# Scoring order of the forget-attention tiles, late rows of the out projections, and a third v buffer

## The chip, the core and the metric

The kernel runs on one core of one Trainium2 chip. The metric is device microseconds of one execution, lower is better. One launch computes both layers; weights, activations and scratch tensors lie in HBM, and everything is moved by DMA that SyncE (SP) issues.

## The reference, cut to what matters

The trunk has 1024 tokens, model width 1024, 16 heads of 64, and two layers.

```
x = x + (fox(h) * silu(gate)) @ w_out      # layer 1, h = rms_norm(x)
x = x + (dsw(h) * silu(gate)) @ w_out      # layer 2
fox:  c = cumsum(log_sigmoid(f_logit));  s = q k^T / 8 + c_i - c_j,  causal softmax, @ v
dsw:  three groups (window, dilation) = (128,1), (512,4), (2048,16): rotary, banded
      softmax in each group, groups combined by the softmax of their log-sum-exps
```

In layer 1 the 128 queries of tile t (t = 0 to 7) see the keys of tiles 0 to t, so tile 7 has eight times the score work of tile 0. In layer 2 a tile sees its own and at most one more tile of keys.

## The kernel before, in words

Each projection multiplies a 128-token tile by a 1024 x 384 weight piece: eight k blocks, each with three matmuls (input high part times weight high part, times weight low part, input low part times weight high part), 24 matmuls in all (`project`, L308 to L316). After every second k block `flow.tick()` runs; a tick is the kernel's clock, here called a **slot**. A tile of a projection is four slots, a head pair (eight tiles) is 32.

TensorE's instructions stay in the order in which the program emits them. What isn't projection is hung on slots by `flow.at(slot, fn)`, and so lands between two pairs of k blocks. The other engines and SP get their order from a planner in the compiler, by priority and by when it expects operands and a free buffer.

Layer 1 runs the gate projections, then eight head pairs (L716 to L743), then the out projection in three column parts (L746 to L772). For a head pair, every two tiles `heads_pair` (L396 to L425) norms q and k, splits them into fp16 high and low parts `hl`, and SP transposes them by DMA into `qk_t`. `fox_tile` (L615 to L691) then scores a tile: matmuls `s` (L442), bias, maximum and copy to `p` on DVE (L644), exp on ACT (L487), fp16 high part on ACT (L490) and low part on POOL (L493) into `ph`, a DMA transpose to `ptt` (L494), and, some slots later, `values`: the matmuls with v (L501 to L503), divided and gated on DVE into `y` (L674, L680), which goes to `y_d` in HBM. Tiles 0 to 3 have one transpose for both heads, tiles 4 to 7 one for each head. There are two `ph` and three `ptt` buffers, four of `p`, two of v (`vt`).

Counted from the first slot of its head pair, tile t is scored at slot 4t+20 (the second head of tiles 4 to 7 two slots later), and its values come 8 slots and then 2 to 4 later (`lpf`, `fox`): in tiles 0 to 3 12 slots after scoring, in tiles 4 to 7 10 slots after the scoring of each head. So the tiles of a head pair are spread evenly in time, whatever their number of keys, and its last ones fall into the next head pair. The next weights are loaded and split meanwhile (`ahead`, L294); a small matmul of theirs (`scale`, L270) is hung on slot 28.

In the last head pair scoring is up to three slots earlier (`ahead`, L602). There the values are multiplied straight into the row buffer `yts[t]`, whose other columns were loaded from `y_d` (`load_y`), and both halves of the row are transposed on TensorE (`y_ready`, `transpose_half`), copied to `xh` by ACT (L325) and to `xl` by DVE (L326), two and three slots after the values. Only then may the out projection of tile t start, at slot 32+4t of the last head pair. Layer 2 ends in the same way.

Of the kernel before, what the change touches and what calls it, by code (L numbers as in the profile page):

```python
# [22 lines left out]
P = 128  # L23
# [59 lines left out]
def trunk(ctx, tc, ins, out, cfg):  # L83
# [56 lines left out]
    par_i = sb.tile([P, P], I32, name="par_i", tag="n2k", bufs=cfg["nb"])  # L140
    nc.gpsimd.iota(par_i, [[1, P]], base=P, channel_multiplier=-1)
    nc.vector.tensor_single_scalar(par_i, par_i, 1, ALU.bitwise_and)
    par = const.tile([P, P], F32, name="par")
    nc.vector.tensor_scalar(par, par_i, NEG, None, ALU.mult)
    nc.gpsimd.affine_select(par, par, [[-1, P]], ALU.is_ge, NEG, base=0, channel_multiplier=1)

# [92 lines left out]
    under = {}  # L239

# [78 lines left out]
    def transpose_half(row, h, t, own=False):  # L319
        pt = ps_o.tile([P, 512], F32, name="pt", tag="o") if own else ps_pj.tile([P, 512], F32, name="pt", tag="pj")  # L320
        for j in range(4):
            nc.tensor.transpose(pt[:, j * P : (j + 1) * P], row[:, j * P : (j + 1) * P], ident)  # L322
        pv = pt.rearrange("p (k s) -> p k s", k=4)
        dh = xh[:, 4 * h : 4 * h + 4, t * P : (t + 1) * P]
        nc.scalar.copy(dh, pv)  # L325
        nc.vector.tensor_sub(xl[:, 4 * h : 4 * h + 4, t * P : (t + 1) * P], pv, dh.bitcast(F32))  # L326
# [69 lines left out]
    def heads_pair(gi, t, hd):  # L396
# [55 lines left out]
    def v_tile(vs):  # L452
        vt = sb.tile([P, NT, 2, 129], F16, name="vt", tag="vt")
# [111 lines left out]
    zt = const.tile([P, NT, NH], F32, name="zt")  # L565

    def forget_logits(t, ps):
# [3 lines left out]
        a = sm.tile([P, NT, NH], F32, name="fa", bufs=1)  # L571
# [28 lines left out]


    def ahead(hp, t):  # L602
        if hp < NHP - 1:
            return cfg["lsf"], cfg["lpf"]
        n = cfg["lsf"] - t // 2
        return n, (22 if t < 4 else 21) - n

    bcs = {}

    def load_bc(hp, h):  # L610
        for e in range(2):
# [3 lines left out]
    def fox_tile(hp, t, gs, kts, vt, e0):  # L615
        LS, LP = ahead(hp, t)
# [8 lines left out]
        def score(e, c):  # L625
            a, b = pieces[c]
            if c == 0:
# [43 lines left out]
        def finish():  # L671
            o = st["o"]
            rec = sm.tile([P, 2], F32, name="rec", tag="rec")
            nc.vector.reciprocal(rec, o[:, :, HD])  # L674
            if hp == NHP - 1:
                y = yts[t][1][:, 384:]
            else:
                y = sb.tile([P, P], F32, name="y", tag="y")
            for e in range(2):
                nc.vector.scalar_tensor_tensor(y[:, e * HD : (e + 1) * HD], o[:, e, :HD], rec[:, e : e + 1], gs[:, e * HD : (e + 1) * HD], ALU.mult, ALU.mult)  # L680
            if hp == NHP - 1:
                y_ready(t, flow.now)
# [4 lines left out]
        ts, tv = cfg["fox"][2 * (hp == NHP - 1) + both]  # L687
# [6 lines left out]
    yts = {}  # L694
    turned = set()

    def load_y(t, g):
        yts[t] = rows2("yt")
        nc.sync.dma_start(yts[t][0], y_d[tile_rows(g, t), :512])
# [311 lines left out]
```

## Time and profile before

| what | value |
|---|---|
| time, median of 3 runs (lowest, highest) | 1839.21 us (1836.2, 1841.85) |
| the profiled execution, and its span | 1839.68 us, 1837.9 us |
| PE busy | 1763.5 us, 96% |
| DVE, ACT, POOL busy | 1097.0, 987.9, 953.1 us (60%, 54%, 52%) |
| chain of waits, by engine | PE 51%, DMA 21%, DVE 9%, issue 7%, POOL 6%, ACT 5% |
| projections L313, x8448 | 2393.4 us of busy time (they overlap) |

PE is TensorE's matmuls, PEld its weight loads, SPq the DMA queue that SP issues. The page's strip of 40 slices shows PE at 9 tenths in almost all of them; the head pairs of layer 1 lie in the fourth to thirteenth slice, where the strip of the DMA engines stands at 7 to 9.

### The profile page before, as it was taken

The page shows a single profiled execution, that of the slowest core. Times are in us where ns is not written, and L with a number is a line of the kernel's source. Part 1 is how long each engine was busy: PE and PEld are TensorE (multiplying, and loading weights), DVE is VectorE, ACT ScalarE, POOL GpSimd, SP SyncE. Part 2 cuts the span into 40 slices and gives each one's busy share as a digit, 9 for nine tenths or more (in the row PEclk, how much of TensorE's full clock was granted, in tenths as well). Part 3 has the DMA queues.
Part 4 walks back from the last instruction along what each step waited for, and adds up shares of the span by engine and source line. Part 5 has one row for each costly group of instructions (what it writes and reads, how often), then busy time and mean ns, then how long its engine had stood idle before and what let it go on. Part 6 is the DMA issues. An engine that isn't in the chain of part 4 may idle for free.

```text
span 1837.9 us, 39161 instructions
## 1 busy us (share of the span) xinstructions
PE 1763.5 (96%) x13784; PEld 1695.6 (92%) x13784; DVE 1097.0 (60%) x3762; ACT 987.9 (54%) x2648; POOL 953.1 (52%) x1163
## 2 busy tenths in 40 slices
PE   6999999999998899999999999999999999999999
PEld 5999889888887889999999999999999999999999
DVE  8546666576654363355555666666666766667641
ACT  6536656566664254455555565555555555555520
POOL 4215555565553121155565655666676766757620
PEclk9999999999999999999999999999999999999999
DMA  8447888888889464356767687667666766668752
GB/s 273 118 127 155 182 174 183 186 168 177 193 185 202 128 221 135 94 123 137 144 129 143 134 201 142 132 157 151 142 148 152 167 143 145 151 133 186 175 168 92
DMA packets 631430, 289.27 MB, mean 157 GB/s; under 512 B 510000, under 2 KB 594992, under 8 KB 631232
## 3 DMA queue, kind: packets, MB, share of 16 engines
q1 hardware_dynamic: 631232, 286.77, 69.2%
q8 instruction: 108, 1.77, 0.4%
q14 instruction: 90, 0.74, 0.1%
HBM read 124.87 MB, written 37.03 MB: 88 GB/s over the span
## 4 chain that ended last, share of the span: by engine, by line
PE 51%; DMA 21%; DVE 9%; issue 7%; POOL 6%; ACT 5%; SPq 2%; POOLq 0%; ACTq 0%; DVEq 0%
PE pj L313 44%; DMA ptt<-ph 6%; DMA raw<-in_w_dsw 4%; PE s L442 3%; DMA raw<-in_w_fox 3%; DMA qk_t<-hl 3%; POOL w L291 2%; DMA x_d<-xo 1%; POOL hl L421 1%; POOL ph L493 1%; DMA og_d<-og 1%; ACT ph L490 1%; DVE w L291 1%; ACT w L289 1%; PE pt L322 1%
## 5 line engine op out<-in xcount | busy, mean ns | idle before, releaser
L313 PE MATMUL pj<-w,xh 128*128 128x384 f32 (+2 forms) x5632 | 1450.9, 340 | 35.7 <-ACT w L289 11.9
L313 PEld LDWEIGHTS pj<-w,xh 128*128 128x128 f32 x5632 | 1004.1, 191 | 48.6 <-ACT w L289 12.9
L313 PE MATMUL pj<-w,xl 128*128 128x384 f32 (+2 forms) x2816 | 942.5, 335 | 0.1
L313 PEld LDWEIGHTS pj<-w,xl 128*128 128x128 f32 x2816 | 537.9, 191 | 0.9 <-DVE xl L326 0.9
L291 POOL TENSOR_TENSOR w<-raw,w 128x384 fp32r<-128x384 f32 (+2 forms) x264 | 265.4, 1026 | 349.3 <-ACT w L289 330.0
L493 POOL TENSOR_TENSOR ph<-p,ph 128x512 f16<-128x512 f32 (+3 forms) x176 | 173.0, 999 | 161.5 <-ACT ph L490 116.4
L289 ACT CAST w<-raw 128x384 fp32r<-128x384 f32 (+2 forms) x352 | 162.6, 500 | 123.0 <-PE pj L313 50.7
L421 POOL TENSOR_TENSOR hl<-u,hl 128x512 f16<-128x512 f32 x128 | 150.9, 1179 | 120.5 <-ACT hl L420 119.7
L823 POOL TENSOR_TENSOR ph<-p,ph 128x768 f16<-128x768 f32 (+2 forms) x96 | 155.5, 1619 | 106.5 <-ACT ph L822 104.0
L376 ACT ACTIVATE sq<-pj 128x256 f32<-128x256 f32 x256 | 97.4, 380 | 188.4 <-DVE u L371 186.8
L442 PE MATMUL s<-qk_t 128*128 128x128 f16 (+1 forms) x1504 | 163.9, 249 | 15.7 <-DMA qk_t<-hl 11.2
L501 PEld LDWEIGHTS <-ptt 128*128 128x128 f16 x1136 | 103.8, 99 | 43.1 <-issue 28.6
L258 DVE TENSOR_REDUCE vm<-raw 128x1 f32<-128x256 f32 x128 | 53.7, 419 | 148.7 <-DMA raw<-in_w_dsw 115.7
L487 ACT ACTIVATE p<-p,acc 128x512 f32<-128x512 f32 (+2 forms) x192 | 108.9, 608 | 56.6 <-DVE acc L644 56.6
L442 PEld LDWEIGHTS <-qk_t 128*128 128x128 f16 x1504 | 109.7, 98 | 32.0 <-DMA qk_t<-hl 14.0
L420 ACT CAST hl<-u 128x512 f16<-128x512 f32 x128 | 79.1, 618 | 102.7 <-DVE u L418 85.5
L490 ACT CAST ph<-p 128x512 f16<-128x512 f32 (+3 forms) x176 | 89.6, 536 | 71.3 <-DMA ptt<-ph 69.4
L371 DVE TENSOR_TENSOR u<-pj,gr 128x256 f32<-128x256 f32 x256 | 106.3, 415 | 19.5 <-PE pj L313 19.5
L818 ACT ACTIVATE p<-p,og 128x128 f32<-128x128 f32 (+1 forms) x256 | 97.5, 441 | 33.2 <-DVE og L817 33.1
L502 PEld LDWEIGHTS <-ptt 128*128 128x128 f16 x1136 | 106.8, 98 | 0.9 <-issue 0.9
L422 DVE COPY hl<-hl 128x512 f16<-128x512 f16 x128 | 67.1, 524 | 66.8 <-POOL hl L421 66.3
L503 PEld LDWEIGHTS <-ptt 128*128 128x128 f16 x1136 | 106.8, 98 | 0.0
(167 smaller groups left out, 2260.6 us busy)
## 6 DMA issues: line engine op xcount, KB each, us to landing
raw<-in_w_dsw SPq DMA_DIRECT2D x96, 384.0 KB, 3.8
raw<-in_w_fox SPq DMA_DIRECT2D x32, 384.0 KB, 3.7
og_d<-og SPq DMA_DIRECT2D x64, 132.0 KB, 3.3
cmb<-og_d SPq DMA_DIRECT2D x64, 132.0 KB, 3.0
bc<-c_d SPq DMA_DIRECT2D x32, 256.0 KB, 5.1
gs_d<-ge SPq DMA_DIRECT2D x32, 192.0 KB, 2.7
xt<-in_xt SPq DMA_DIRECT2D x16, 256.0 KB, 4.4
xrow<-in_x SPq DMA_DIRECT2D x16, 256.0 KB, 4.5
```

The source lines that it names most:

```text
L289: nc.scalar.copy(w[:, 0, :n], raw[:, k % 2, :n])
L291: eng.tensor_sub(w[:, 1, :n], raw[:, k % 2, :n], w[:, 0, :n].bitcast(F32))
L313: nc.tensor.matmul(ps[:, :n], a[:, k, cols], w.slabs[k][:, j, :n], start=(k == 0 and i == 0), stop=(k == KT - 1 and i == 2))
L371: nc.vector.tensor_mul(u[:, t % 2].rearrange("p (a b) d -> p a b d", a=2), ps[:, : 4 * HD].rearrange("p (a b d) -> p a b d", a=2, b=2), gr ...
L421: nc.gpsimd.tensor_sub(hl[:, :, :4, 1], u, hl[:, :, :4, 0])
L442: nc.tensor.matmul(s[:, c0 : c0 + cnt * P].rearrange("p (c s) -> p c s", c=cnt), qk[:, i, blk], kk[:, j : j + cnt, e], start=(h == 0), sto ...
L487: nc.scalar.activation(p, p, AF.Exp, bias=acc, scale=-1.0)
L490: nc.scalar.copy(ph[:, e, 0, cols], p)
L493: (nc.gpsimd if pool_l else nc.vector).tensor_sub(ph[:, e, 1, cols], p, ph[:, e, 0, cols])
L502: nc.tensor.matmul(o[:, e, :HD], hi, vt[:, j, e, :HD], start=False, stop=False, skip_group_check=True)
L503: nc.tensor.matmul(o[:, e, :], lo, vt[:, j, e, HD:], start=False, stop=(b == n - 1), skip_group_check=True)
L823: nc.gpsimd.tensor_sub(ph[:, 1], st["p"], ph[:, 0])
```

## The change

Tiles of layer 1 are scored at slots out of a table, `due`, in the order 0, 1, 4, 2, 5, 3, 6, 7 with 4, 2, 4, 2, 4, 4, 8 and 4 slots behind each; in the last head pair all are at 4t+20, with values 8 slots and then 2 to 4 later, as elsewhere. Each tile loads its own piece of the gate (`gsf`), three buffers of one tile in place of three of two. The DMA transpose of q and k is put four slots behind the arithmetic. The rows of `c` (`bc`) are loaded at other slots.

Rows of the earlier head pairs are loaded and transposed ahead (`turn_y`, seven of eight blocks, PSUM from the pool of the attention outputs); the last head pair's block is transposed alone (`turn_last`), and `project` demands it only before its last two k blocks. `vt` gets a third buffer. Layer 2 has three `qk_t` buffers in place of four, the mask `par` is built at the start of layer 2, and two small tiles share another's buffers.

```diff
-    def project(w, cols):
+    def project(w, cols, last=None):
         for k in range(KT):
+            assert k < KT - 2 or last is None or last in turned
@@ heads_pair
-        qk_t = lay([P, 12, P], F16, name="qk_t", tag="qk_t")
-        nc.sync.dma_start_transpose(qk_t, hl.rearrange("p i a b d -> p (i a b d)"))
-        return qk_t.rearrange("p (i a) s -> p i a s", i=2)
+        def turn():
+            qk_t = lay([P, 12, P], F16, name="qk_t", tag="qk_t")
+            nc.sync.dma_start_transpose(qk_t, hl.rearrange("p i a b d -> p (i a b d)"))
+            return qk_t.rearrange("p (i a) s -> p i a s", i=2)
+        return turn
@@ v_tile
-        vt = sb.tile([P, NT, 2, 129], F16, name="vt", tag="vt")
+        vt = lay([P, NT, 2, 129], F16, name="vt", tag="vt")
@@ fox_tile
+            if e == 0 and c == 0:
+                gs = st["gs"] = lay([P, P], F32, name="gsf", tag="gsl")
+                nc.sync.dma_start(gs, gs_d[t * P : (t + 1) * P, hp * P : (hp + 1) * P])
...
             if hp == NHP - 1:
-                y_ready(t, flow.now)
+                turn_last(y, t, flow.now + 2)
...
-                urgent(lambda e=e, c=c: score(e, c), "ps", e0 + LS + ts[e * len(pieces) + c])
-            urgent(lambda e=e: values(e), "pv", e0 + LS + LP + tv[e])
+                urgent(lambda e=e, c=c: score(e, c), "ps", sl + ts[e * len(pieces) + c])
+            urgent(lambda e=e: values(e), "pv", sl + LP + tv[e])
+    def turn_y(t, g, slots):
+        for h, (n, (s0, s1)) in enumerate(zip((4, 3), slots)):
+            def load(h=h, n=n, s1=s1):
+                yt = lay([P, 512], F32, name="yt", tag="ga")
+                nc.sync.dma_start(yt[:, : n * P], y_d[tile_rows(g, t), 512 * h : 512 * h + n * P])
+                flow.at(s1, lambda: transpose_rows(yt, 4 * h, n, t, True))
+            flow.at(s0, load)
+    def turn_last(y, t, s):
+        def go():
+            transpose_rows(y, KT - 1, 1, t)
+            turned.add(t)
+        flow.at(s, go)
@@ loop over head pairs
-                    kts.append(heads_pair(0, t - 1, hd))
+                    turn = heads_pair(0, t - 1, hd)
+                    flow.at(flow.now + 4, lambda turn=turn, kts=kts: kts.append(turn()))
-                    fox_tile(hp, t - 1 + i, gsl[:, i], kts, vt, flow.now - 4 + 4 * i)
+                    fox_tile(hp, tt, kts, vt, s0 + (cfg["due"][tt] if hp < NHP - 1 else 4 * tt + 20))
             if hp == NHP - 1:
-                flow.at(flow.now + sum(ahead(hp, t)) - 3, lambda t=t: load_y(t, 0))
+                a = max(flow.now + 6, s0 + cfg["due"][t] - 4 * NT + cfg["lpf"] + 9)
+                turn_y(t, 0, [(a, a + 6), (a + 2, a + 8)])
@@ CFG
+ bc=((1, 0, 26), (1, 1, 28), (0, 0, 38), (0, 1, 46)), due=(29, 33, 39, 45, 35, 41, 49, 57)
- lsd=(..., (12, 9)), l1=dict(..., qk_t=6), l2=dict(..., qk_t=4, og=3)
+ lsd=(..., (12, 10)), ty2=((0, 4), (1, 5)), l1=dict(..., qk_t=6, vt=3, gsl=3)
+ l2=dict(..., qk_t=3, og=3, vt=3, gsl=3, par=1)
```

## Rows read from the trace of the kernel before

**Rows 1.** The page's first part: engine, busy us, share, instructions.

```profile
PE 1763.5 (96%) x13784; PEld 1695.6 (92%) x13784; DVE 1097.0 (60%) x3762; ACT 987.9 (54%) x2648; POOL 953.1 (52%) x1163
```

**Rows 2.** Stretches: length; busy PE, PEld, DVE, ACT, POOL; granted clock, DMA share, GB/s.

```profile
112.00:488.00 376.00, 354.75 (x3284) 332.49 (x3283) 239.37 (x846) 227.49 (x571) 206.79 (x206) 0.97 0.82 171
488.00:549.00 61.00, 58.40 (x561) 53.75 (x559) 36.87 (x129) 39.57 (x98) 37.13 (x39) 0.97 0.85 188
549.00:605.00 56.00, 47.03 (x442) 40.99 (x441) 30.33 (x97) 24.05 (x50) 17.77 (x19) 0.94 0.88 184
...
785.00:1745.00 960.00, 945.42 (x7226) 920.20 (x7225) 618.89 (x2269) 538.25 (x1549) 610.19 (x812) 1.00 0.70 149
```

**Rows 3.** Waits of PE, 112 to 488 us: total us, times, longest.

```profile
PE o L501 <- DMA ptt<-ph: 10.7, 6, 3.9
PE s L442 <- DMA qk_t<-hl: 6.2, 6, 2.8
PE s L442 <- DVE acc L644: 4.2, 6, 2.4
```

**Rows 4.** Timeline of PE: start, us, what, idle before it and its releaser.

```profile
225.90 0.94 PE L442 MATMUL s<-qk_t 128*128 128x256 f16 x8 [1.81 <-DMA qk_t<-hl]
...
255.84 0.24 PE L501 MATMUL o<-vt,ptt 128*128 128x65 f16 x1 [3.88 <-DMA ptt<-ph]
...
424.35 0.20 PE L501 MATMUL o<-vt,ptt 128*128 128x65 f16 x1 [1.80 <-DMA ptt<-ph]
```

**Rows 5.** Timeline of PE: the matmul that is hung on slot 28.

```profile
257.15 0.35 PE L270 MATMUL pj<-vm,ones 128*128 128x4 f32 x1
```

**Rows 6.** Stretches behind the three gaps of rows 4, with the granted clock.

```profile
224.00:228.00 4.00, 2.19 (x20) 2.03 (x17) 2.65 (x11) 3.42 (x10) 1.88 (x3) 1.00 0.82 172
...
254.00:262.00 8.00, 6.16 (x45) 5.92 (x46) 4.66 (x21) 3.72 (x9) 2.62 (x3) 0.57 0.61 142
...
424.00:430.00 6.00, 5.65 (x49) 5.56 (x50) 4.57 (x22) 4.31 (x11) 3.22 (x3) 0.72 0.44 103
```

**Rows 7.** Waits of ACT, 112 to 605 us, and its timeline near 570 us.

```profile
ACT ph L490 <- DMA ptt<-ph: 69.4, 42, 3.8
...
570.13 1.03 ACT L490 CAST ph<-p 128x512 f16<-128x512 f32 x2 [3.77 <-DMA ptt<-ph]
...
571.07 1.06 ACT L325 CAST xh<-pt 128x512 fp32r<-128x512 f32 x2
```

**Rows 8.** The stretch ahead of the gap at 255.84 us.

```profile
240.00:247.00 7.00, 7.00 (x91) 6.64 (x88) 2.27 (x12) 3.49 (x8) 3.31 (x4) 1.00 1.15 228
```

**Rows 9.** Transposes of the probabilities, line L494.

```profile
DMA to landing us min/median/max: 2.3/3.7/7.2
```

**Rows 10.** Waits of PE, 488 to 605 us.

```profile
PE pj L313 <- ACT xh L325: 3.9, 1, 3.9
PE pj L313 <- DVE xl L326: 3.2, 1, 3.2
PE s L442 <- DMA qk_t<-hl: 2.8, 2, 2.6
PE pt L322 <- DVE yt L680: 1.1, 1, 1.1
PE pt L322 <- DVE u L418: 0.5, 1, 0.5
```

**Rows 11.** Timeline of DVE ahead of the wait for `xl`.

```profile
596.61 0.75 DVE L196 TENSOR_SCALAR rt<-rt_pf 128x24 f32<-128x24 f32 x8 [0.19 <-issue]
...
599.16 0.68 DVE L326 TENSOR_TENSOR xl<-pt,xh 128x512 fp32r<-128x512 f32 x1
```

**Rows 12.** Waits of SP's queue over the span.

```profile
SPq L731 <- DVE y L680: 12.5, 7, 2.3
```

**Rows 13.** The chain that ended last: one tile of a projection.

```profile
804.34 4.22 PE pj L313 x24
```

**Rows 14.** Waits of PE in layer 2, 785 to 1745 us.

```profile
PE pj L313 <- DVE u L418: 6.3, 7, 1.3
```

More of the change, by code (lines that the diff above doesn't have):

```diff
@@ L319, in transpose_half, with transpose_rows @@
     def transpose_half(row, h, t, own=False):
+        transpose_rows(row, 4 * h, 4, t, own)
+    def transpose_rows(row, k0, n, t, own=False):
         pt = ps_o.tile([P, 512], F32, name="pt", tag="o") if own else ps_pj.tile([P, 512], F32, name="pt", tag="pj")
-        for j in range(4):
+        for j in range(n):
             nc.tensor.transpose(pt[:, j * P : (j + 1) * P], row[:, j * P : (j + 1) * P], ident)
-        pv = pt.rearrange("p (k s) -> p k s", k=4)
-        dh = xh[:, 4 * h : 4 * h + 4, t * P : (t + 1) * P]
+        pv = pt[:, : n * P].rearrange("p (k s) -> p k s", k=n)
+        dh = xh[:, k0 : k0 + n, t * P : (t + 1) * P]
         nc.scalar.copy(dh, pv)
-        nc.vector.tensor_sub(xl[:, 4 * h : 4 * h + 4, t * P : (t + 1) * P], pv, dh.bitcast(F32))
+        nc.vector.tensor_sub(xl[:, k0 : k0 + n, t * P : (t + 1) * P], pv, dh.bitcast(F32))
     def inv_sqrt(y, v, n, a):
@@ L564, in trunk @@
     nc.sync.dma_start(bfb, b_f.partition_broadcast(P))
-    zt = const.tile([P, NT, NH], F32, name="zt")
+    zt = lay([P, NT, NH], F32, name="zt", tag="p")
     def forget_logits(t, ps):
@@ L570, in forget_logits @@
             return
-        a = sm.tile([P, NT, NH], F32, name="fa", bufs=1)
+        a = lay([P, NT, NH], F32, name="fa", tag="p")
         nc.vector.scalar_tensor_tensor(a, zt, -1.0, zt, ALU.mult, ALU.max)
@@ L598, in urgent, with load_bc, fox_tile @@
         flow.at(slot, go)
[L602 to L606, printed above, removed]
     bcs = {}
-    def load_bc(hp, h):
-        for e in range(2):
+    def load_bc(hp, h, es=(0, 1)):
+        for e in es:
             bcs[hp, e, h] = lay([P, 512], F32, name="bc", tag="ga")
             nc.sync.dma_start(bcs[hp, e, h], c_d[2 * hp + e, h * 512 : (h + 1) * 512].partition_broadcast(P))
-    def fox_tile(hp, t, gs, kts, vt, e0):
-        LS, LP = ahead(hp, t)
+    def fox_tile(hp, t, kts, vt, sl):
+        LP = cfg["lpf"]
         nk = (t + 1) * P
@@ L674, in finish @@
             nc.vector.reciprocal(rec, o[:, :, HD])
+            y = sb.tile([P, P], F32, name="y", tag="y")
+            for e in range(2):
+                nc.vector.scalar_tensor_tensor(y[:, e * HD : (e + 1) * HD], o[:, e, :HD], rec[:, e : e + 1], st["gs"][:, e * HD : (e + 1) * HD], ALU.mult, ALU.mult)
             if hp == NHP - 1:
[L676 to L680, printed above, removed]
@@ L694, in trunk @@
[L694 to L699, printed above, removed]
-        nc.sync.dma_start(yts[t][1][:, :384], y_d[tile_rows(g, t), 512 : D - P])
-    def y_ready(t, s):
-        def go(h):
-            transpose_half(yts[t][h], h, t)
-            if h == 1:
-                del yts[t]
-                turned.add(t)
-        for h in range(2):
-            flow.at(s + 2 + h, lambda h=h: go(h))
+                urgent(lambda e=e, c=c: score(e, c), "ps", sl + ts[e * len(pieces) + c])
@@ L720, in trunk @@
             load_bc(0, 0)
-        flow.at(s0 + ahead(hp, NT - 1)[0] + 5, lambda hp=hp: load_bc(hp, 1))
-        if hp + 1 < NHP:
-            flow.at(s0 + 20, lambda hp=hp: load_bc(hp + 1, 0))
+        for h, e, slot in cfg["bc"]:
+            if hp + 1 - h < NHP:
+                flow.at(s0 + slot, lambda n=hp + 1 - h, h=h, e=e: load_bc(n, h, (e,)))
         kts = []
@@ L789, in dsw_pair @@
     def dsw_pair(g, t0, qks, vt, done, get, LSD, LPD):
-        mask = par if g == 2 else None
+        mask = masks.get(g)
         look, at = [], [0]
@@ L864, in combine @@
         t0 = t - CB + 1
+        y2 = lay([P, N2, HD], F32, name="y2", tag="gsl")
+        nc.vector.tensor_mul(y2, y, gv)
         if hp == NHP - 1:
             for i in range(CB):
-                nc.vector.tensor_mul(yts[t0 + i][1][:, 384:].rearrange("p (e d) -> p e d", e=2), y[:, 2 * i : 2 * i + 2], gv[:, 2 * i : 2 * i + 2])
-                y_ready(t0 + i, flow.now + 2 * i)
-        else:
-            y2 = sb.tile([P, N2, HD], F32, name="y2", tag="gsl", bufs=cfg["gb"])
-            nc.vector.tensor_mul(y2, y, gv)
+                turn_last(y2.rearrange("p (t e) d -> p t (e d)", e=2)[:, i], t0 + i, flow.now + 3 + i)
+        else:
             nc.sync.dma_start(
@@ L882, in load_cmb @@
         assert all((hp, g, i) in written for g, i in [(0, i) for i in range(NT)] + [(2, t // 2), (2, t // 2 + 4)])
[L883 removed]
+        cmb[1] = lay([P, CB, P], F32, name="gsd", tag="gsl")
         for gg in range(2):
@@ L942, in trunk @@
                     for i in range(2):
-                        flow.at(flow.now + LSD + LPD - 3 + 2 * i, lambda t=t0 + i: load_y(t, 1))
+                        turn_y(t0 + i, 1, [(flow.now + a + 2 * i, flow.now + b + 2 * i) for a, b in cfg["ty2"]])
         w = w2
```

35 lines of the change are left out of this document (17 added, 18 removed).

## The prediction

> **What bounds the kernel now.** I read the page's first part, then a table of stretches, then the waits of PE in each stretch, then the timeline at the longest gaps. The reader is to see four things.
>
> First, PE is the bound: 96% of the span is matmuls [rows 1], so this change can only win back PE's gaps and what a gap costs behind it. The stretches say where they are [rows 2]. The head pairs of layer 1 but the last (112 to 488 us) have 376.00 - 354.75 = 21.3 us of gaps; the last (488 to 549) 2.6; the first part of the out projection (549 to 605), into which the attention's tail reaches, 9.0; and layer 2 (785 to 1745) only 14.6 in 960.
>
> Second, a gap is paid twice in layer 1. The granted clock, 1.00 in layer 2, is 0.97, 0.97 and 0.94 in those three stretches. It has two levels, 2.4 and 1.2 GHz, so a mean of 0.97 over 376 us means 0.03 x 376 = 11.3 us of matmul time lost (the rounding of the column leaves 2 us either way); 0.03 x 61 = 1.8 and 0.06 x 56 = 3.4 in the others. Behind the gap at 255.84 us, 3.88 us long, the clock is 0.57 over 8 us: 0.43 x 8 = 3.4 us more [rows 4, 6]. In all 32.6 + 4.4 + 12.4 = 49.4 us can be won back.
>
> Third, the gaps of the first stretch have three releasers: transposed probabilities 10.7 us, six times, about once for each head pair; transposed q and k 6.2; and the score's PSUM tile, held until DVE has copied it out, 4.2 [rows 3]. Which tile is late follows from the slots. Behind the gap at 255.84 us come attention matmuls with v and then, at 257.15, the small matmul that is hung on slot 28 [rows 4, 5]; at that slot the code has the values of tile 7 of the pair before, second head (50 + 8 + 2 - 32 = 28). The gap at 225.90, ahead of eight score matmuls, is tile 6's (four 256-column matmuls, then two of 256 and two of 128, for seven blocks of keys; the listing merges them): it wants the keys that left the projection 12 slots earlier.
>
> Fourth, why they are late. ACT waits 69.4 us, 42 times, to write `ph` because its two buffers still sit in a transpose [rows 7]; the longest landing of one is 7.2 us against a median of 3.7 [rows 9]. In 240 to 247 us, ahead of the longest gap, the DMA share is 1.15 while DVE is busy 2.27 of 7 us [rows 8]; over the head pairs it is 0.82 [rows 2]. So the chain behind the scores is full for part of each head pair and slack for the rest.
>
> **The change part by part.** *The scoring order.* Let the chain serve 36 key blocks in 32 slots, 1.125 a slot (the average it must serve). Before, tile t brings t+1 blocks every four slots: the backlog right after tiles 4, 5, 6, 7 is 5, 6.5, 9 and 12.5 blocks, the last worth 11.1 slots. Values of these tiles come 10 slots after scoring, so tile 7 alone is late, by a slot; the gap at slot 28 is such a one. After, in the order 0, 1, 4, 2, 5, 3, 6, 7 the backlogs are 4.8, 2.3, 5, 3.5, 7.3, 6.8, 9.3 and 8.3 blocks: at most 8.2 slots. I let 9.7 of the 10.7 us go. Tile 6's keys get 17 slots in place of 12; but tile 4's now get 11 in place of 12, and their transpose is put four slots later in SP's order, into slots 28 to 31, where tile 7's transposes are. Two thirds go: 4.1 of 6.2. Waits on the copies from PSUM fall by half, as light tiles come between heavy ones: 2.1 of 4.2. Together 15.9 of 21.1, three quarters; the same share of the clock loss is 8.5. Term: -24.4, bounds -32.6 and 0; how it could lose is the last rival.
>
> Of the clock I take the average, and a rule says it isn't sure. A gap of 1.81 us was free (clock 1.00 behind it), one of 1.80 us was charged 0.28 x 6 = 1.7 us [rows 4, 6]. The Trainium skill, "TensorE: Matmul & The Clock Gate", section "Part 1: The HAM clock gate", has the gate watch activity on a free-running beat, so that equal gaps may fare differently. If this holds, gaps that shrink may keep their charge; that is the first rival.
>
> *The last head pair and the out projection.* In the last head pair I change nothing: its own tiles keep one every four slots, behind the late tiles 6 and 7 of the pair before. In 549 to 605 us two waits are 7.1 of 8.9 us [rows 10], and both are in-order queues: ACT reaches the copy to `xh` at 571.07 only after a `ph` copy that sat 3.77 us behind a transpose [rows 7]; DVE reaches `xl` at 599.16 after the rotary tables, from 596.61 on [rows 11]. After, each tile has one such hand-over in place of two, with a quarter of the columns: transpose at slot 4t+34, wanted before the last k block. Between them lie nine matmuls, 9 x 4.22 / 24 = 1.6 us [rows 13]; the first half now has one slot, 1.06 us. The queues ahead are the same, so an unlucky one still costs. I halve the three waits on `xh`, `xl` and `yt`, 8.2 us, and the clock loss: -4.1 - 1.7. Against it, tail tiles are scored two or three slots later: by the same count the backlog at tile 7 is 18.4 blocks, not 15.9. Values ran there without a wait for a transpose, so the tail serves at least 1.5 a slot (15.9 in about 10 slots); 2.5 blocks more are 1.7 slots, 1.8 us. Term: -4.0, bounds -12.4 and +6 (another wait like the one at 571 us, 3.9, with its share of the clock, 1.7).
>
> *At nothing.* The third `vt` buffer: values of tile 7 now reach slot 69, past the start of the pair after next at 64; without it that pair's v would wait. PE shows no wait for it in layer 1 before [rows 3], so nothing is gained either. The gate loads and the other split rows cost SP and ACT instructions; ACT is busy 227.49 of 376 and 24.05 of 56 us [rows 2], and gates are wanted 10 slots after they are issued. If that cover fails it is the slow rival below. The mask leaves the first microseconds for the end of the gate projections, where it has a layer's length of slack. Three `qk_t` in layer 2: a pair of tiles is scored 16 slots after its heads and serves as keys eight slots later, so its buffer is free at 24, when the fourth pair asks. The largest wait of PE in layer 2, 6.3 us, is for DVE reading out PSUM [rows 14], which no part touches. Layer 2: 0, with 4 either way for the planner's new order, under the 14.6 us of gaps there.
>
> **Sum.** -24.4 - 4.0 = -28.4, from 1839.7 for the profiled execution, 0.5 above the median of the runs: 1811.3, so 1811 us. If a gap goes, nothing else is late next but PE itself.
>
> **The rivals.** *Gaps shrink, the clock stays low.* Half of the first stretch's 21.3 us goes, none of the 11.3, and the tail gives 3: 1839.7 - 10.6 - 3 = 1826. For it: 1.80 us was enough to be charged. Against: most waits have a clear cause that goes.
>
> *All of it goes.* First stretch and tail: 1839.7 - 32.6 - 12.4 = 1795. Against: tile 4's keys have a slot less.
>
> *Order doesn't matter.* If the chain is bound by its sum (two `ph` buffers in use through the whole head pair), spreading gives nothing and only the tail moves: 1838. For it, 42 waits on `ph` [rows 7]; against, a DMA share of 0.82 on average.
>
> *Slower: gate loads block SP.* With the new table four tiles are under way at slots 39 to 45 (1, 4, 2, and 0 or 5), and a gate buffer is held from scoring to the values; there are three. A load whose buffer is still held waits at the head of SP's queue, and all transposes behind it wait too: two slots for tile 2 (39 to 41, when tile 0's values are through), four for tile 5 (to 45), two each for tiles 3 and 6, ten in all. A slot is about 56 / 32 = 1.7 us there. If half of them are lost ahead of tile 5's and 3's transposes, values come 7.3 + 5 - 10 = 2.3 slots late: 4 us and 1.7 of clock in each of seven head pairs, 40 us, against 24.4 + 4.0 gained: 1851. It decides if SP loses over about three slots a head pair. For it: SP already waits 12.5 us for gate buffers [rows 12]. Against: the planner may put the transposes ahead of the load, since the gate is wanted 10 slots later.
>
> **How the numbers follow.** Forecast 0.50; gaps shrink 0.20; all goes 0.10; order doesn't matter 0.07; slower 0.13. The forecast's own range, with the bounds of its terms, is 1801 to 1822. Down to 1795 and up to 1834 the range takes in the first two rivals and leaves out the last two, 2 in 10. About 0.3%, 5.5 us, can be told from no change: faster 0.50 + 0.20 + 0.10 = 0.80, within 0.07, slower 0.13.
>
> **What would show it.** Right: from the first to the seventh head pair PE waits for transposed probabilities at most twice, not six times; gaps there near 5 us and the clock at 0.99; in the out projection's first part one gap over 2 us at most. Wrong: SP waiting over 2 us at the gate load in most head pairs (slower); waits of `s` for `qk_t` once a head pair at tile 4; many gaps of 1 to 2 us with the clock still at 0.97 (gaps shrink); or ACT's wait for `ph` unchanged near 69 us with PE's gaps as before (order doesn't matter). Gaps in layer 2 beyond 19 us would say that its buffers were not free after all.

## The result, and the profile after

The changed kernel takes 1827.26 us (median of 7 runs, 1826.13 to 1831.49) against 1841.85 us (7 runs of the kernel before beside it): ratio 0.9929, 95% interval 0.9912 to 0.9946. It is faster, by some 13 us. The forecast was 28.4 us: the sign was right, the size less than half. The median of the kernel before went from 1831 to 1842 us from chip to chip, so from here on kernels are compared by their ratio to the kernel before on the same chip.

The page's first part of the profiled execution after (1826.89 us, span 1825.1), to set beside [rows 1]:

```profile
PE 1755.6 (96%) x13784; PEld 1689.7 (93%) x13784; DVE 1103.3 (60%) x3774; ACT 988.5 (54%) x2664; POOL 953.9 (52%) x1163
```

The stretches that answer to [rows 2]: length; busy PE, PEld, DVE, ACT, POOL; granted clock, DMA share, GB/s.

```profile
112.00:480.00 368.00, 348.31 (x3237) 326.14 (x3235) 243.80 (x839) 224.04 (x563) 205.58 (x203) 1.00 0.87 172
480.00:541.00 61.00, 57.80 (x560) 52.74 (x561) 41.05 (x132) 43.34 (x105) 35.98 (x36) 0.97 0.98 201
541.00:597.00 56.00, 48.84 (x508) 44.64 (x507) 30.64 (x101) 25.37 (x59) 21.52 (x23) 0.93 0.90 197
775.00:1735.00 960.00, 948.23 (x7252) 922.12 (x7250) 620.86 (x2278) 542.39 (x1561) 610.51 (x813) 1.00 0.70 151
```

The reader is to see that the head pairs still have 368.00 - 348.31 = 19.7 us of gaps (21.3 before), but that their clock is 1.00 and no longer 0.97. The tail's clock is as low as before. A window with nearly the same work in both says it more exactly: from the first arithmetic on q and k of the first head pair to that of the eighth. First before, then after:

```profile
122.00:493.10 371.10, 349.85 (x3268) 327.38 (x3267) 235.48 (x839) 224.98 (x566) 206.36 (x206) 0.97 0.83 173
```

```profile
123.00:485.20 362.20, 342.41 (x3220) 319.83 (x3220) 239.63 (x833) 221.96 (x561) 204.68 (x204) 1.00 0.88 174
```

Seven head pairs take 371.1 - 362.2 = 8.9 us less. Of these 349.85 - 342.41 = 7.4 are PE's busy time, and only 1.5 are gaps. Not all of the 7.4 is the clock: with the later slots more of the seventh head pair's attention falls behind the window, 39 value matmuls and 14 score matmuls, and 5 more projection matmuls lie in it. At the 0.03, 0.09 and 0.18 us that such matmuls stand apart in PE's timeline, that is some 1.5 us (an estimate), which leaves 6 for the clock. The span is 12.8 us shorter: 1.0 is lost ahead of this window; the tail from there to the first gate projection of layer 2 gives 3.1 (PE starts that one 11.0 us earlier, at 672.82 us for 683.78, and the eighth head pair's arithmetic 7.9 earlier); layer 2 gives 1.8.

Which waits made the gaps? PE's waits in 112 to 480 us after, to set beside [rows 3]:

```profile
PE o L504 <- DMA ptt<-ph: 11.5, 10, 1.9
PE s L445 <- DVE acc L642: 5.0, 10, 1.0
```

The wait for transposed q and k is gone (6.2 before). The wait for transposed probabilities is not: 11.5 us in ten pieces, after 10.7 in six. It was cut into shorter pieces. Who waited for `ptt`, after, over the whole span (total us, times):

```profile
ACT ph L493: 61.4, 36
...
PE o L504: 14.3, 11
```

Before, ACT's number was 69.4 [rows 7], so the ring of `ph` buffers is nearly as crowded as it was. Two gaps in PE's timeline, and the stretches that hold them (the granted clock is the third number from the end), show what shorter pieces can save:

```profile
368.87 0.20 PE L504 MATMUL o<-vt,ptt 128*128 128x65 f16 x1 [1.94 <-DMA ptt<-ph]
...
480.10 0.24 PE L504 MATMUL o<-vt,ptt 128*128 128x65 f16 x1 [2.78 <-DMA ptt<-ph]
```

```profile
366.00:376.00 10.00, 7.12 (x87) 6.39 (x86) 5.59 (x19) 5.66 (x16) 4.61 (x6) 1.00 1.03 218
476.00:484.00 8.00, 5.22 (x45) 4.65 (x44) 3.48 (x11) 3.17 (x10) 3.57 (x5) 0.79 1.02 211
```

Behind 1.94 us the clock stays at 1.00; behind 2.78 it falls to a mean of 0.79 over 8 us, another 1.7 us. Length alone doesn't decide. In e15_ypj (below), whose head pairs have the same code, the same wait was 1.91 us long and was charged 0.21 x 8 = 1.7 us:

```profile
368.60 0.20 PE L504 MATMUL o<-vt,ptt 128*128 128x65 f16 x1 [1.91 <-DMA ptt<-ph]
```

```profile
368.00:376.00 8.00, 7.40 (x80) 7.10 (x81) 3.85 (x18) 5.74 (x16) 4.64 (x5) 0.79 0.91 221
```

Yet short pieces come off better on the whole. In the changed kernel and in nine runs below that keep its order and two `ph` buffers (e2, e3, e4, e5, e7, e8, e9, e15, e16), PE's longest wait in 112 to 480 us is 1.5 to 2.9 us and the clock is 1.00, in e15_ypj 0.99; in e1_even, with waits up to 4.1 us, it is 0.97. So what the change gained in the head pairs it gained mostly on the clock, with shorter gaps, and hardly on the gaps themselves.

PE's waits in the tail, 480 to 600 us, to set beside [rows 10]:

```profile
PE pt L321 <- DVE xl L325: 3.9, 3, 3.5
PE pt L321 <- issue: 2.8, 2, 1.6
PE o L504 <- DMA ptt<-ph: 2.8, 1, 2.8
PE pj L309 <- DVE xl L325: 2.5, 1, 2.5
PE pt L321 <- DMA yt<-y_d: 1.1, 1, 1.1
```

The two waits of 7.1 us on `xh` and `xl` are one of 2.5, but the rows transposed ahead have waits of their own (`pt`, 7.8 us).

### The profile page after: what moved, and what is told of

The parts are those of the page before. It is cut to its first block, busy times and chain, and to the rows that moved or that the text cites. A ratio compares the mean times of both kernels' runs of the same rounds, so it can differ in the third digit from the quotient of the medians.

```text
span 1825.1 us, 39283 instructions
## 1 busy us (share of the span) xinstructions
PE 1755.6 (96%) x13784; PEld 1689.7 (93%) x13784; DVE 1103.3 (60%) x3774; ACT 988.5 (54%) x2664; POOL 953.9 (52%) x1163
## 4 chain that ended last, share of the span: by engine, by line
PE 53%; DMA 17%; DVE 10%; ACT 7%; POOL 6%; issue 5%; SPq 1%; POOLq 0%; DVEq 0%; ACTq 0%
PE pj L309 47%; DMA raw<-in_w_dsw 4%; DMA ptt<-ph 4%; PE s L445 3%; POOL w L285 2%; DMA raw<-in_w_fox 2%; POOL ph L496 2%; DMA qk_t<-hl 2%; DVE p L642 2%; POOL hl L420 1%; ACT p L490 1%; DMA x_d<-xo 1%; ACT ph L493 1%; PE pt L321 1%; DVE u L417 1%
## 5 line engine op out<-in xcount | busy, mean ns | idle before, releaser
L504 PEld LDWEIGHTS <-ptt 128*128 128x128 f16 x1136 | 103.6, 98 | 44.3 <-issue 25.1
L388 DVE TENSOR_REDUCE pj<-sq 128x8 f32<-128x512 f32 x128 | 88.4, 691 | 47.5 <-ACT sq L375 47.4
L370 DVE TENSOR_TENSOR u<-pj,gr 128x256 f32<-128x256 f32 x256 | 106.5, 416 | 11.4 <-PE pj L309 11.2
L421 DVE COPY hl<-hl 128x512 f16<-128x512 f16 x128 | 61.7, 482 | 78.7 <-POOL hl L420 78.6
L505 PEld LDWEIGHTS <-ptt 128*128 128x128 f16 x1136 | 106.3, 97 | 1.8 <-issue 1.8
```

What stands on the lines that cost most here:

```text
L370: nc.vector.tensor_mul(u[:, t % 2].rearrange("p (a b) d -> p a b d", a=2), ps[:, : 4 * HD].rearrange("p (a b d) -> p a b d", a=2, b=2), gr ...
L504: nc.tensor.matmul(o[:, e, :], hi, vt[:, j, e, HD:], start=(b == 0), stop=False, skip_group_check=True)
L505: nc.tensor.matmul(o[:, e, :HD], hi, vt[:, j, e, :HD], start=False, stop=False, skip_group_check=True)
```

## The experiments

Each was timed against the kernel before in five rounds. The texts quoted name theories by letters: A, the order of scoring is what gains; B, it is worth nothing; C, the values are merely asked for too early; E, the transposes of q and k stand ahead of late probabilities in SP's order; J, other engines serve q and k in between as well; H, SP's queue is the limit; I, the DMAs' bytes are; K, the new tail is worth little; D, M and N, the number of buffers of `ph`, `ptt` or `p` is the limit. L stands for two things: in e11_ph3 to e13_p6 the serial work behind the scores, in e15_ypj the copies on DVE.

**The order alone.** Every tile of layer 1 is scored at the old slots again, all else as after.

```diff
- due=(29, 33, 39, 45, 35, 41, 49, 57)
+ due=(20, 24, 28, 32, 36, 40, 44, 48)
```

> The changed kernel with one part undone: tiles of all head pairs are scored evenly again (due = 20, 24, ..., 48); the split rows, the late transposes of q and k and the third v buffer stay. Theory A (the order is what raised the clock from 0.97 to 1.00 and closed the waits for q and k): back to about 1838, waits of s for qk_t of some 6 us and a clock near 0.97 in the head pairs. Rival B (the late transposes of q and k did it, by freeing SP's queue): stays at 1827 +- 3, no qk_t waits, clock 1.00.

Ratio 0.9988 (0.9976 to 1.0001): nearly all of the gain is gone. PE's waits, 112 to 480 us:

```profile
PE s L445 <- DMA qk_t<-hl: 14.8, 6, 4.1
PE s L445 <- DVE acc L642: 4.7, 5, 1.5
PE o L504 <- DMA ptt<-ph: 4.1, 3, 3.4
```

The order is worth 0.6%, about 11 us, and A stands. What returns is not the wait for probabilities but that for keys, in six long pieces, and more of it than before the change (6.2); here the transposes of q and k are asked for four slots later. From the first arithmetic on q and k to that of the eighth head pair it is

```profile
124.00:501.10 377.10, 351.21 (x3280) 328.86 (x3279) 235.81 (x838) 225.93 (x566) 204.75 (x206) 0.97 0.81 169
```

so 377.1 us, where the kernel before takes 371.1 and the changed one 362.2. Undoing the order alone thus gives a kernel that is 6 us worse there than the one before, and the 0.6% holds that too. The new order with the transposes at their old place was not tried.

**Later values.** In all head pairs but the last, values come two slots later, and the rows are read back two slots later.

```diff
-        LP = cfg["lpf"]
+        LP = cfg["lpf"] + (2 if hp < NHP - 1 else 0)
-                a = max(flow.now + 6, s0 + cfg["due"][t] - 4 * NT + cfg["lpf"] + 9)
+                a = max(flow.now + 6, s0 + cfg["due"][t] - 4 * NT + cfg["lpf"] + 11)
```

> The changed kernel with the values of all head pairs but the last two slots later (10 and then 2 to 4 behind scoring), and the rows read back two slots later. Theory C (the chain behind a score keeps up, but its latency for tile 7 is a slot or so over the 10 it has): PE's waits for transposed probabilities, 14.3 us in the changed kernel, fall under 4, and the time to about 1818. Rival D (the chain cannot serve more: two ph buffers): the waits return at the new slots, 10 us or more, 1827 +- 3.

Ratio 0.9978 (0.9965 to 0.9992), slower than the changed kernel. PE's waits, 112 to 480 us:

```profile
PE s L445 <- DMA qk_t<-hl: 10.0, 6, 2.0
PE s L445 <- DVE acc L642: 7.6, 10, 1.6
PE o L504 <- DMA ptt<-ph: 0.7, 3, 0.3
```

The wait for probabilities went as C has it, and 12.6 us came back in the two others: 18.3 us in all, 16.5 after. The seven head pairs take what they took, 360.3 us from 123.1 to 483.4, so C, by which the time falls to 1818, falls. So does D, if its returning waits are those for probabilities. What makes this kernel slower lies behind: from the eighth head pair's first arithmetic to layer 2's first gate projection, first after, then here:

```profile
485.20:672.80 187.60, 171.12 (x1480) 160.97 (x1480) 106.36 (x327) 96.10 (x234) 68.38 (x70) 0.96 0.81 195
```

```profile
483.40:681.90 198.50, 176.14 (x1507) 164.12 (x1507) 106.94 (x331) 98.20 (x236) 69.02 (x70) 0.95 0.76 187
```

The waits that moved when their due time was moved fit a chain with too little room better than a due time set too early; that it is the buffers, held two slots longer, is not shown here.

**Keys later in SP's order.** The transposes of q and k are put 7 slots behind the arithmetic, not 4.

```diff
-                    flow.at(flow.now + 4, lambda turn=turn, kts=kts: kts.append(turn()))
+                    flow.at(flow.now + 7, lambda turn=turn, kts=kts: kts.append(turn()))
```

> The changed kernel with the DMA transpose of q and k seven slots behind the arithmetic in place of four, so that SP reaches tile 7's transposes (scored at slot 25) before those of the third pair of tiles (heads at slot 24). Theory E (tile 7's first transpose sits about 3 us behind the transpose of q and k in SP's queue): the waits for transposed probabilities fall from 14.3 to under 7 us; tile 4's keys may come late in exchange, up to 2 us a head pair; 1820 to 1830. Rival D (two ph buffers are the limit): those waits stay at 10 us or more, 1827 or slower.

Ratio 0.9923 (0.9906 to 0.9941), waits of 11.1 and 4.7 us: as after. The planner left the transposes of q and k where they were in SP's order (at 361.19 us, ahead of a `ptt` at 364.25), so this doesn't test E, and it stays open. In the changed kernel a block of tile 7 is complete at 361.33 us (POOL's low part), and SP issues its transpose only at 364.55, behind one of q and k that begins at 361.55.

**Other DMAs off SP.** Loads of the gate and of the bias rows and stores of `y` are issued by ACT.

```diff
-                nc.sync.dma_start(gs, gs_d[...])
+                nc.scalar.dma_start(gs, gs_d[...])
... (so too the loads into bcs and the stores of y)
```

> The changed kernel with the gate loads, the y stores and the bias loads of layer 1's head pairs issued by ACT in place of SP, so that SP's queue holds the transposes and the weight loads alone (some 40 of its 128 us of issue time in 160 us go); the bytes are the same. Theory H (SP's queue, in order and busy issuing for 80% of the head pairs, is what makes the transposed probabilities late): PE's waits in 112 to 480 us fall from 16.5 to under 8 and the time by 6 to 10 us, to about 1819. Rival D (two ph buffers) and rival I (the DMA engines, share 0.92): waits within 3 us of 16.5, 1827 +- 3.

Ratio 0.9977 (0.9958 to 0.9996), slower than after; waits for probabilities 10.8 us, for the copies out of PSUM 10.6 (5.0 after). SP was relieved, but by less than was taken off it: added up over its DMA instructions in 270 to 430 us, it issues for 96 us and not for 120, where the loads and stores that left had taken 33. The transposes of probabilities took longer to issue, 71 us and not 57. Their rows there (ns min/median/max), first after, then here:

```profile
L497 SPq DMA_TRANSPOSE ptt<-ph x35: 1207/1425/3118, 272.0 to 426.1; - x35
```

```profile
L497 SPq DMA_TRANSPOSE ptt<-ph x35: 1190/1962/3618, 274.2 to 428.2; - x35
```

With a fifth less to issue PE waits no less, so H falls. What makes this kernel slower was not found.

**No bias loads.** Every head pair uses the bias rows that were loaded for the first, so this kernel leaves 14 of 16 heads' rows out.

```diff
-            if hp + 1 - h < NHP:
+            if hp + 1 - h < 1:
-            nc.vector.tensor_tensor_reduce(p, ..., bcs[hp, e, a // 512][...], ...)
+            nc.vector.tensor_tensor_reduce(p, ..., bcs[0, e, a // 512][...], ...)
```

> The changed kernel without the bias loads after the first head pair (the rows of c of head pair 0 are used for all, so the outputs are not the reference's): 28 loads of 256 KB, a tenth of the head pairs' bytes, and a twentieth of SP's issue time go. Theory I (the DMA engines are the limit): a tenth less to move makes room of 5 us a head pair, so PE's waits there fall from 16.5 to under 6, 1815 to 1819. Theory H (SP's queue): a third of that, waits near 13. Rival D (two ph buffers): nothing, 1827 +- 3.

Ratio 0.9931 (0.9915 to 0.9946), waits for probabilities 11.8 us. The stretch 270 to 430 us of this kernel has a DMA share of 0.86, where the changed kernel has 0.93:

```profile
270.00:430.00 160.00, 150.74 (x1500) 140.15 (x1500) 106.73 (x379) 100.83 (x252) 94.40 (x93) 1.00 0.86 164
```

Fewer bytes and nothing gained: I falls.

**One more buffer of each ring.** These kernels use the first head's bias row for all heads, so the other rows are left out, which frees 4 KB of each partition. The first is their base, each of the others spends the room on one ring.

```diff
- l1=dict(ga=7, ptt=3, ph=2, p=4, ...)
+ l1=dict(ga=5, ptt=3, ph=2, p=4, ...)   # e10_room
+ l1=dict(ga=5, ptt=3, ph=3, p=4, ...)   # e11_ph3
+ l1=dict(ga=5, ptt=4, ph=2, p=4, ...)   # e12_ptt4
+ l1=dict(ga=5, ptt=3, ph=2, p=6, ...)   # e13_p6
```

> Ground for the three kernels run with it: the changed kernel with one bias row block of head pair 0 and head 0 used for all heads (outputs not the reference's), so that five buffers of that tag do in place of seven and 4 KB a partition are free, unused here. All theories: PE's waits in the head pairs as without the bias loads, 19 +- 3 us in 112 to 480 us, and 1820 to 1830.

> The same with a third ph buffer in the 4 KB. Theory D (the two ph buffers, each held from the high part's copy to the landing of its transpose, are what limits the chain behind the scores): ACT's wait for ph falls from 43 us to under 15, PE's waits for transposed probabilities from 12 to under 4, and the time by 6 to 12 us against the kernel with the room unused. Rival L (what limits it is the serial work between score and landing, DVE, ACT, POOL and SP in turn, which more buffers don't shorten): PE's waits within 3 us, time within 3.

> The same with a fourth ptt buffer in the 4 KB in place of a third ph. Theory M (SP holds transposes back because PE has not read the third last one yet; it waits 7 us for that in 112 to 480 us): those 7 us go, and PE's waits fall by 4 to 7. Theory D (ph) and rival L (serial work): within 3 us of the kernel with the room unused.

> The same with six p buffers in place of four in the 4 KB. Theory N (scores leave PSUM late because the four p buffers of a heavy tile are held until POOL has written its low part): PE's waits of s for the copy, 5 to 8 us in 112 to 480 us, fall under 2, and tile 7's chain starts earlier, so the waits for transposed probabilities fall too, under 6; 5 us or more faster than with the room unused. Theories D and M and rival L: within 3 us.

Base 0.9943 (0.9926 to 0.9960); third `ph` 0.9867 (0.9848 to 0.9885), 14 us under the base; fourth `ptt` 0.9888 (0.9870 to 0.9907), 10 us under it; six `p` 0.9942 (0.9926 to 0.9957), nothing. D and M both hold, N falls. Who waited for `ptt`, in the base, with a third `ph`, and with a fourth `ptt`:

```profile
ACT ph L493: 63.8, 35
...
PE o L504: 11.5, 10
```

```profile
PE o L504: 8.7, 10
...
ACT ph L493: 3.2, 3
```

```profile
ACT ph L493: 73.0, 46
...
PE o L504: 5.8, 8
```

ACT's wait for `ph` nearly goes with the third `ph`, and grows with the fourth `ptt`, yet both gain: ACT's wait is a sign of the full ring, not its price. With the fourth `ptt` it is SP that no longer waits for the values to release a `ptt` (10.1 us in the base, no such wait there). One block more under way between exp and values is what pays, in either ring. Neither theory was right to the letter: by D the fourth `ptt` should have done nothing, and PE's wait should have fallen under 4 us with the third `ph`, where 8.7 are left. The profiles of base and third `ph`, 9.0 us apart, show 5.0 of it in the seven head pairs (359.3 to 354.3) and 7.9 in the tail; the rest of the kernel loses 3.9.

**A third `ph` with nothing left out.** The room comes once from one `p` and one buffer of the 2 KB row ring, once from one `p` and the third v buffer.

```diff
- nb=3, l1=dict(ga=7, ptt=3, ph=2, p=4, qk_t=6, vt=3, gsl=3)
+ nb=2, l1=dict(ga=7, ptt=3, ph=3, p=3, qk_t=6, vt=3, gsl=3)   # e14_ph3full
+ nb=3, l1=dict(ga=7, ptt=3, ph=3, p=3, qk_t=6, vt=2, gsl=3)   # e17_ph3vt2
```

> The changed kernel with a third ph buffer in layer 1 and nothing left out: the room comes from one p buffer (three) and one buffer of the 2 KB row ring (two). Theory D (two ph buffers limit the chain): ACT's wait for ph between 112 and 475 us, 43 us after, nearly goes, and the ratio to before is 0.985 to 0.989, some 10 us under the changed kernel. Theory I' (the third buffer helped only because the bias loads were gone): the ratio stays within 0.991 to 0.995. A loss against the changed kernel (above 0.996) would say that the smaller rings are needed.

> The changed kernel with a third ph buffer and nothing left out; here the room comes from the third v buffer and one p buffer (three). Theory D: as e14, 0.985 to 0.990, if the third v buffer is of little worth; if e16 is slower than the changed kernel, this one loses the same. Rival I': 0.992 or more whatever v does.

Ratios 0.9889 (0.9871 to 0.9907) and 0.9863 (0.9846 to 0.9880): I' falls. The second is 1811.76 us against 1835.05 and beats both kernels: the whole change with the room for the third v buffer given to `ph`. Who waited for `ptt` there, and the window from the first head pair to the eighth, to set beside the changed kernel's above:

```profile
PE o L504: 5.0, 11
...
ACT ph L493: 0.2, 1
```

```profile
123.00:475.40 352.40, 341.01 (x3229) 318.47 (x3228) 231.19 (x831) 223.27 (x561) 202.97 (x203) 1.00 0.91 178
```

Against the changed kernel the seven head pairs are 362.2 - 352.4 = 9.8 us shorter: 8.4 of gaps (19.8 to 11.4) and 1.4 of busy time. The waits for probabilities that lie in this window fell from 14.3 to 5.0 us. By the ratio this kernel is some 25 us faster than the one before, near the 28 that I had forecast without the buffer; but 11.4 us of gaps in the head pairs are twice the 5 that I had forecast, and in its profile 8.0 of the 14.9 us to the changed kernel lie in layer 2, where nothing was changed (see layer 2 below).

**Two v buffers.** The third one of layer 1 alone is taken away.

```diff
- qk_t=6, vt=3
+ qk_t=6, vt=2
```

> The changed kernel with two v buffers in layer 1 again, as before the change. If the third buffer is needed by the later values (tile 7's reach slot 69, past the next use at 64): PE waits for the projection of v once a head pair, some 1 to 3 us each, ratio 0.997 or more. If not (PE showed no wait of this kind, and the values of the last tiles end before the projection's copy is asked for): the ratio is that of the changed kernel, 0.992 to 0.994.

Ratio 0.9923 (0.9906 to 0.9940), as the changed kernel: the third v buffer does nothing that can be measured.

**The old order with a third `ph`**, that is e17_ph3vt2 with the old slots.

```diff
- due=(29, 33, 39, 45, 35, 41, 49, 57)
+ due=(20, 24, 28, 32, 36, 40, 44, 48)
```

> e17 (third ph buffer, two v buffers, three p) with the old even scoring order of layer 1. Theory D1 (ring and peak are two limits): the order still counts, because tile 7 still brings its eight blocks at once and its keys are wanted early: waits for transposed probabilities or keys return, some 5 us or more with the clock, ratio 0.989 to 0.993 against 0.9863 for e17. Rival D2 (the ring alone was the limit; with three buffers either order fits): the ratio is that of e17, 0.985 to 0.988.

Ratio 0.9976 (0.9961 to 0.9992). PE's waits, 112 to 475 us:

```profile
PE o L504 <- DMA ptt<-ph: 19.0, 10, 3.8
PE s L445 <- DVE acc L642: 5.1, 10, 0.8
PE s L445 <- DMA qk_t<-hl: 1.4, 4, 0.9
```

With the old order the third buffer is worth at most a little (0.9988 to 0.9976, overlapping intervals), with the new one 0.7%: D1. Here ACT hardly waits for `ph` (5.9 us) and probabilities are late nonetheless: each of the ten waits stands ahead of eight sets of value matmuls, and only tile 7 has eight. The window of the seven head pairs says the same without the rest of the kernel:

```profile
123.70:499.60 375.90, 347.68 (x3262) 324.24 (x3261) 231.27 (x838) 225.15 (x566) 204.22 (x206) 0.98 0.84 170
```

With the old order it is 377.1 us with two `ph` (e1_even) and 375.9 with three, with the new one 362.2 and 352.4: the third buffer is worth 1 us there with the old order, and 10 with the new.

**Scores first.** The planner's priority of the scores is raised, in both layers, in the changed kernel and in e17_ph3vt2.

```diff
- ps=0
+ ps=100
```

> The changed kernel with the planner's priority of the scores and what follows them raised to that of the q and k arithmetic. Theory J (tile 7's probabilities are late because POOL, ACT and SP serve the q and k of tiles 4 and 5 in between, 3 us in SP's queue alone): the waits for transposed probabilities fall from 14.3 to under 6; waits for q and k may come in exchange; time 1818 to 1824. Rivals D, H, I (a resource is full): the sum of the waits stays within 4 us of 16.5, whichever releaser they have; 1827 +- 3.

> e17 with the priority of the scores raised in the planner (as in e7). If the head pairs again end some 4 us earlier and the tail does not give it back, ratio 0.984; if, as in e7, the tail gives it back, the ratio stays at 0.986. A loss is possible: with three buffers the chain is not late, and scores put ahead of the projections only move the gaps (0.988).

Ratios 0.9929 (0.9910 to 0.9948) and 0.9919 (0.9896 to 0.9942). In the first the eighth head pair's arithmetic starts at 480.31 us, not 485.19, and the tail gives all of it back; PE waits 10.9 us for probabilities in 112 to 480 us, so J falls. The second loses against e17_ph3vt2 (0.9863): PE's waits for the copies out of PSUM in 112 to 475 us are 13.5 us there, and 6.1 in e17_ph3vt2.

**The tail.** First the last head pair and its out projection as before the change; then the new one with its transposes of the rows read back in the projections' PSUM, at the end of layer 2 too.

```diff
-                turn_last(y, t, flow.now + 2)
+                y_ready(t, flow.now)                              # e9_oldtail
... (with the old slots, load_y and y_ready as before)
-                flow.at(s1, lambda: transpose_rows(yt, 4 * h, n, t, True))
+                flow.at(s1, lambda: transpose_rows(yt, 4 * h, n, t, False))   # e15_ypj
```

> The changed kernel with the last head pair of layer 1 as before: its tiles scored up to three slots earlier, whole rows transposed in two halves after the values, out projection tiles starting only then; the order in the other head pairs stays, and layer 2 ends as in the changed kernel. My prediction's step (the late rows alone win 4 us): 1831. Rival K (the transposes of the rows read back cost as much as the late rows win): 1827 +- 1.5, with gaps of 9 to 12 us between 480 and 600 us in either kernel.

> The changed kernel, but the last head pair's transposes of y take PSUM from the projections' ring instead of the attention outputs' ring. Theory K (these transposes wait for a ring that the attention holds): the waits of pt and pj in 480 to 600 us, about 10 us after, fall by half, ratio 0.990 or less. Rival L (they wait for the copies on DVE, whichever ring): waits and time unchanged, 0.992 to 0.994; or, with the projections held up, slower.

Ratios 0.9940 (0.9922 to 0.9958) and 0.9940 (0.9922 to 0.9959): neither can be told from the changed kernel's 0.9929. PE's waits in the tail, first with the old one (480 to 605 us), then with the other PSUM (480 to 600):

```profile
PE o L504 <- DMA ptt<-ph: 7.9, 2, 5.2
PE pj L309 <- DVE xl L325: 5.2, 2, 4.5
PE s L445 <- DMA qk_t<-hl: 1.8, 2, 1.6
```

```profile
PE pt L321 <- DMA yt<-y_d: 3.2, 2, 2.7
PE pj L309 <- DVE xl L325: 3.0, 1, 3.0
PE pt L321 <- DVE xl L325: 2.8, 1, 2.8
PE o L504 <- DMA ptt<-ph: 2.8, 2, 2.5
```

By the ratios the new tail is worth 2 us, and their intervals allow anything from a loss of 3 to a gain of 7, so neither my step (4 us) nor K (nothing) is decided. Its waits for `xl` don't depend on the ring: L stands.

**Layer 2 with its old buffers** (`qk_t=4`, two `vt`).

```diff
- l2=dict(..., qk_t=3, og=3, vt=3, gsl=3, par=1)
+ l2=dict(..., qk_t=4, og=3, vt=2, gsl=3, par=1)
```

> The changed kernel with layer 2's buffers as before: two of v and four of q and k (layer 1 keeps three of v). Theory F (the third v buffer is what layer 2 gained, some 2.9 us): 1830, with PE's gaps in layer 2 back from 11 to about 14 us. Rival G (the gain there is the planner's new order, not a buffer): 1827 +- 1.5.

Ratio 0.9945 (0.9927 to 0.9963), not to be told from the changed kernel; its gaps in 775 to 1735 us are 12.1 us, after 11.8, before 14.6. So the old buffers don't bring the gaps back. Nor need the 1.8 us that layer 2 gave have a cause in the change. Layer 2 has the same code in the changed kernel and in all runs but this one, e7, e14, e15 and e19, and from its first gate projection to the end of the span their profiles show 1144 to 1152 us. Two of them, first after, then e17_ph3vt2:

```profile
672.82:1825.10 1152.28, 1134.93 (x8473) 1106.43 (x8472) 683.49 (x2421) 601.14 (x1697) 643.22 (x848) 1.00 0.64 145
```

```profile
665.84:1810.16 1144.32, 1132.57 (x8473) 1106.61 (x8472) 686.39 (x2421) 601.33 (x1697) 643.93 (x848) 1.00 0.64 146
```

Whether that goes with the kernel or with the execution is not known. A difference of a few us between whole profiles can come from there; the windows of the head pairs are free of it.

## Why the prediction was half right

**The step that failed** is "I let 9.7 of the 10.7 us go". I took the chain from exp to values for a server: so many key blocks a slot, ten slots of time, and only the peak of the backlog counts. By that count no tile was late in the new order. Yet PE waits 11.5 us for probabilities (14.3 up to 485.2 us), and every one of these waits stands, as before the change, ahead of tile 7's values. The chain also has room for two blocks of probabilities between ACT's copy and the transpose's landing, and for three from there to the values, and that limit is in force when the peak is gone. It could have been counted from the profile. A head pair has 12 transposes of probabilities (96 in layer 1). The fifth one takes 54 us, so two `ph` buffers let each block be held 2 x 54 / 12 = 9 us on average. From ACT's copy to the landing, with copies and transposes of the second to seventh head pair matched in program order, a block is held 7.8 us on average, before and after: the ring is in use some 87% of the time, and it is full where the long ones are. Tile 7's are held 11.5 us on average after (9.7 before). One of them, worked on in the fifth head pair, is copied by ACT from 357.19 us on and read by PE from 368.87 on, 11.7 us later; in e17_ph3vt2 its like is copied at 353.02 and read at 364.99, 12.0 us, where a head pair takes 53 us and three buffers allow 3 x 53 / 12 = 13. The block isn't quicker with the third buffer; nobody waits for it to leave. These are two single blocks and an estimate; the runs with a third `ph` or a fourth `ptt` carry the point.

The profile had said so: ACT's 42 waits for `ph` [rows 7] were named in the rival "order doesn't matter", at 0.07. I read the mean DMA share of 0.82 against it, but the share is no measure of how long a buffer is held: no bias loads after the first head pair (share 0.86 for 0.93) changed nothing. The rival was half right: its mechanism limits the new order, while e1_even shows that the order matters all the same. The two limits stand one behind the other. Counted from e1_even, the order alone gives 0.6%, the third buffer alone 0.1% (not to be told from nothing), both 1.25%; in the seven head pairs 15, 1 and 25 us of 377. (The kernels with the third buffer have one `p` and one v buffer less; e16_vt2 and e13_p6 say that v and `p` count for little.)

**The other terms.** *Keys*: 4.1 of 6.2 forecast, all went. *Copies from PSUM*: 2.1 of 4.2 forecast; they are 5.0. *Clock in the head pairs*: 8.5 forecast, some 6 by the windows of nearly equal work. It was coupled to the sum of the gaps in the working, and it came almost without them, as they got shorter: in 112 to 480 us 19.7 us of gaps are left and none is charged. The first rival, by which gaps shrink and keep their charge, had the mechanism reversed, though its 1826 is where the time came out. Which gap is charged is in part luck: 1.80 us before [rows 6] and 1.91 in e15_ypj were, 1.94 after was not. The Trainium skill, "TensorE: Matmul & The Clock Gate", section "Part 1: The HAM clock gate", has the gate watch activity in a free-running window; gaps of one length that fare differently agree with that. *The last head pair*: -4.0 forecast, -3.1 seen, of which e9_oldtail can't show that it is not zero. The two hand-overs that I halved did get shorter; the rows transposed ahead wait for `xl`, for `yt` and at issue, which I had at nothing. *The third v buffer*: nothing, as forecast (e16_vt2). *Layer 2*: 1.8 us, inside its 4 either way and inside what its like code differs by. *The slow rival*, gate loads that block SP: SP waits 2.5 us in all at the gate load, at most 1.5 at a time. Its price was also added up wrongly: 7.3 blocks are 6.5 slots, so values would come 1.5 slots late, not 2.3, which makes some 30 us lost and 1841, about the time before. *The range*: the bounds of the two terms add up to 1795 to 1846, so 1801 to 1822 doesn't follow from them, and the time lies outside it. *What would show it*: the clock came (1.00), "at most twice" did not (ten times), nor gaps near 5 us; no wait for tile 4's keys.

## What to carry to other kernels

When a stage is late, count both its peak against its rate and, for each ring, how long a buffer is held against buffers times period over uses, and count the longest blocks as well as the average: here 7.8 us against 9 looked like room, and the late tile's 11.5 were not. A wait of the engine that fills the ring is a sign that the second limit may bind, and no price. If moving the due time only moves the wait to another place, look for a buffer before you look for a better slot. When kernels differ by less than 1%, compare windows of the stage that was changed: layer 2 differed here by up to 8 us with the same code. Where gaps can't be closed, cutting a long one into short ones may still save what the clock charges for it.

## What the runs showed of the hardware

SP's issue of a DMA transpose isn't a fixed cost: with SP's other DMAs moved to ACT's queue the median for the probabilities rose from 1.43 to 1.96 us, while that for q and k fell from 2.06 to 1.41. So a queue that looks full gets emptier by less than is taken from it: 33 us left SP, and its issuing fell by 24, from 120 to 96 us in 160. And 19.7 us of gaps in 368 us, none over 1.94 us, left the granted clock at 1.00, where 21.3 us with pieces up to 3.9 us had left 0.97; a single gap of 1.91 us was charged 1.7 us in one kernel, and one of 1.94 us nothing in another.
